# Larger load tiles for a row-projection and running-record kernel: 64 KB per partition in three slots instead of 48 KB in four

## The chip, the cores and the metric

The kernel runs on one core of one Trainium2 chip. The metric is device time in microseconds (us). The kernel before takes 631.44 us, the median of the six runs beside the changed kernel (631.24 to 631.77). All runs quoted here were of the state "fast". A packet is what one of the core's 16 DMA engines moves in one piece; here a partition's share of a tile is one packet (40 tiles of 128 partitions are the 5120 packets below). Where a number comes from the trace's DMA packet records and not from a printed view, I say so.

## The reference

```python
B, S, D = 8, 2048, 4096
def reference(x, w):                       # x [8, 2048, 4096], w [4096, 1], float32
    proj = (x @ w).squeeze(-1)             # [8, 2048]
    cm = np.maximum.accumulate(proj, axis=1)
    is_record = (proj >= cm).astype(np.float32)
    return np.cumsum(is_record, axis=1).astype(np.float32)
```

Every one of the 268 MB of `x` is used once, in a dot product of 4096 elements.

## The kernel before

The 2048 positions are cut into five groups of 384 (R = 3 rows for each of 128 partitions) and a tail of 128. For a group, eight tiles are loaded, one for each batch row. A tile is 128 partitions x 48 KB, and a partition's three rows lie side by side in memory. Four slots hold tiles. VectorE does the dot over columns 0 to 2816; GpSimd multiplies the other 1280 columns and ACT (ScalarE) sums them. TensorE turns the sums into one row per batch row, in PSUM, and VectorE scans that row.

```python
R = 3; NS = 4; NG = (S - P) // (R * P)
xbuf = [xall[:, i * R * D : (i + 1) * R * D] for i in range(NS)]
for k in range(NK):                                   # NK = NG * B tiles
    g, t = divmod(k, B)
    i = SY.dma_start(out=xbuf[k % NS], in_=x[B - 1 - t, g * N : (g + 1) * N, :]
            .rearrange("(p r) d -> p (r d)", r=R)).then_inc(xs[k % NS], 16)
    if k >= NS:
        i._wait_ge(fr[k % NS], 2 * (k // NS))         # VectorE and ACT are done with the slot
    # ... cut: weights, output of the group before
with V.Fori(0, NG):                                   # GpSimd and ACT have such loops too
    group_scans()
    V.sem_inc(psr, -3)
    V.sem_inc(od, -16)
    for t in range(B):
        b, s = B - 1 - t, t % NS
        V.wait_ge(xs[s], 16).then_inc(go, 1)
        V.sem_inc(xs[s], -16)
        for j in range(R):
            i = dot(xbuf[s][:, j * D : j * D + VC], w_v[:, :VC],
                    sum_v[:, j * B + b : j * B + b + 1])
        i.then_inc(fr[s], 1)
# ... cut: matmuls of each group; the tail: six whole rows, then nine ever smaller pieces
```

Of the kernel before, what the change touches and what calls it, by code (L numbers as in the profile page):

```python
# [13 lines left out]
ALU = mybir.AluOpType  # L14
ACTF = mybir.ActivationFunctionType
NEG = -3.0e38
LOW = -3.2e38
# [3 lines left out]
def kernel(  # L21
# [16 lines left out]
    P = 128  # L38
    B, S, D = x.shape
    WC = 512  # L40
    NW = D // WC
    R = 3
    NS = 4
    NG = (S - P) // (R * P)
    N = R * P
    S0 = NG * N
    assert S0 + P == S and B % NS == 0
    VC = 2816
    PC = D - VC
    CV = 3584  # L50
# [20 lines left out]
    def sb(shape, name, **kw):  # L71
        return pool.tile(shape, FP32, name=name, **kw)
# [5 lines left out]
    xbuf = [xall[:, i * R * D : (i + 1) * R * D] for i in range(NS)]  # L78
    w_sb = sb([P, PC], "w_sb")
    cm = sb([B, N], "cm")  # L80
    rec = sb([B, N], "rec")
    cnt = sb([B, N], "cnt")
    cm_l, rec_l, cnt_l = (sb([B, P], n) for n in ("cm_l", "rec_l", "cnt_l"))
    w_v = wpool.tile([P, CV], FP32, name="w_v")
    ps = wpool.tile([P, WC], FP32, name="ps")
    w_row = w2[:NW, :]
# [8 lines left out]
    sum_v, sum_p = cut(R * B), cut(R * B)  # L95
# [3 lines left out]
    acc_v, acc_p = accs[:, : len(PIECES)], accs[:, len(PIECES) :]  # L99
    fin = cut(1)  # L100
    neg = cut(1)[:B]
    zero = ps[:B, WC - 1 :]

    ns = iter(range(1000))

    def sem(name):
        return tc.alloc_semaphore(f"{name}_{next(ns)}")

    rows = [b for b in reversed(range(B)) if b > 1]
    xs = [sem("xs") for _ in range(NS)]  # L110
    fr = [sem("fr") for _ in range(NS)]
    xt = [sem("xt") for _ in rows]
    xq = [sem("xq") for _ in PIECES]
    ws, idn, bw, wc, cs, od, oe, psr, pd, pl, go, sd, pa, con = (
# [5 lines left out]
    def dot(xsl, wsl, dst):  # L120
        return V.tensor_tensor_reduce(  # L121
            out=xsl, in0=xsl, in1=wsl, scale=1.0, scalar=0.0,
            op0=ALU.mult, op1=ALU.add, accum_out=dst,
        )
# [7 lines left out]
        assert W2 <= c0 and c1 <= W2 + WC  # L132
        return w2[:, c0 - W2 : c1 - W2]

    def scans(cm_, rec_, cnt_, n, cm0, cnt0, base=1):
        V.tensor_tensor_scan(  # L136
            out=cm_, data0=ps[:B, :n], data1=neg.to_broadcast([B, n]), initial=cm0,
            op0=ALU.max, op1=ALU.max,
        )._wait_ge(psr, base).then_inc(psr, 1)
        V.tensor_tensor(  # L140
            out=rec_, in0=ps[:B, :n], in1=cm_, op=ALU.is_ge
        )._wait_ge(psr, base + 1).then_inc(psr, 1)
        V.tensor_tensor_scan(  # L143
            out=cnt_, data0=rec_, data1=zero.to_broadcast([B, n]), initial=cnt0,
            op0=ALU.add, op1=ALU.add,
        )._wait_ge(psr, base + 2).then_inc(cs, 1)

    NK = NG * B
    with tc.tile_critical(no_gpsimd_drain=True):  # L149

        for k in range(NK):
            g, t = divmod(k, B)
            i = SY.dma_start(
                out=xbuf[k % NS],
                in_=x[B - 1 - t, g * N : (g + 1) * N, :].rearrange(
                    "(p r) d -> p (r d)", r=R
                ),
            ).then_inc(xs[k % NS], 16)
            if k >= NS:
                i._wait_ge(fr[k % NS], 2 * (k // NS))  # L160
            if k == 0:
                A.dma_start(
                    out=w_row, in_=w.rearrange("(k c) one -> k (c one)", k=NW)
                ).then_inc(ws, 16)
            if t == NS and g:
                SY.dma_start(
                    out=out[:, (g - 1) * N : g * N], in_=cnt
                )._wait_ge(cs, g + 1).then_inc(od, 16)

        def slot(m):  # L170
            return m // R, xbuf[m // R][:, (m % R) * D : (m % R + 1) * D]

        freed = set()

        def row_load(m, c0, c1, b, done):
            s, xb = slot(m)
            i = SY.dma_start(
                out=xb[:, c0:c1], in_=x[b, S0:, c0:c1]
            ).then_inc(done, 16)
            if s not in freed:  # L180
                freed.add(s)
                i._wait_ge(fr[s], 2 * (NK // NS))

        for m, b in enumerate(rows):
            row_load(m, 0, D, b, xt[m])
        for i, (b, c0, c1, _, _) in enumerate(PIECES):
            row_load(B - 1 - b, c0, c1, b, xq[i])
            if i == 3:
                SY.dma_start(
                    out=out[:, (NG - 1) * N : S0], in_=cnt  # L190
                )._wait_ge(cs, NG + 1).then_inc(oe, 16)


# [10 lines left out]
        for n, k in enumerate(order):  # L204
            c = k * WC
# [16 lines left out]
        V.memset(cnt[:, N - 1 :], 0.0)  # L222
        V.wait_ge(con, 3)
        V.wait_ge(wc, 3)
        V.memset(ps[:B, :N], LOW)  # L225
        V.memset(zero, 0.0).then_inc(psr, 1)

        def group_scans():
            V.wait_ge(od, 16)
            scans(cm, rec, cnt, N, cm[:, N - 1 :], cnt[:, N - 1 :])  # L230

        with V.Fori(0, NG):
            group_scans()
            V.sem_inc(psr, -3)
            V.sem_inc(od, -16)
            for t in range(B):
                b, s = B - 1 - t, t % NS
                V.wait_ge(xs[s], 16).then_inc(go, 1)
                V.sem_inc(xs[s], -16)  # L239
                for j in range(R):  # L240
                    i = dot(
                        xbuf[s][:, j * D : j * D + VC], w_v[:, :VC],
                        sum_v[:, j * B + b : j * B + b + 1],
                    )
                i.then_inc(fr[s], 1)

        G.wait_ge(wc, 3)
        with G.Fori(0, NG):
            for t in range(B):
                s = t % NS  # L250
                for j in range(R):
                    xl = xbuf[s][:, j * D + VC : (j + 1) * D]
                    i = G.tensor_mul(out=xl, in0=xl, in1=w_sb).then_inc(pl, 1)  # L253
                    if j == 0:
                        i._wait_ge(go, 1)
                G.sem_inc(go, -1)  # L256

        with A.Fori(0, NG):
            for t in range(B):
                b, s = B - 1 - t, t % NS  # L260
                for j in range(R):
                    i = add_up(
                        xbuf[s][:, j * D + VC : (j + 1) * D],
                        sum_p[:, j * B + b : j * B + b + 1],
                    )._wait_ge(pl, j + 1)
                i.then_inc(fr[s], 1)
                A.sem_inc(pl, -R)
            A.wait_ge(pd, 1)
            A.sem_inc(pd, -1)

        for g in range(NG):
            for j in range(R):
                for k, l in enumerate((sum_p, sum_v)):
                    i = T.matmul(  # L274
                        out=ps[:B, j:N:R], lhsT=l[:, j * B : (j + 1) * B],
                        rhs=identity, start=k == 0, stop=k == 1,
                    )
                    if j == k == 0:
                        i._wait_ge(fr[NS - 1], 2 * (g + 1) * B // NS)
                    if j == R - 1:  # L280
                        i.then_inc((pd, psr)[k], 1)


# [3 lines left out]
        def piece(xb, v, p, dst_v, dst_p, landed):  # L287
            nonlocal nv, npool, na
            dot(xb[:, v[0] : v[1]], w_v[:, v[0] : v[1]], dst_v)._wait_ge(
                landed, 16  # L290
            ).then_inc(sd, 1)
            nv += 1
            if p:
                xl = xb[:, p[0] : p[1]]
                G.tensor_mul(out=xl, in0=xl, in1=w_pool(*p))._wait_ge(  # L295
                    landed, 16
                ).then_inc(pl, 1)
                npool += 1
                add_up(xl, dst_p)._wait_ge(pl, npool).then_inc(pa, 1)
                na += 1  # L300

        for m, b in enumerate(rows):
            piece(
                slot(m)[1], (0, VC), (VC, D), st_v[:, b : b + 1], st_p[:, b : b + 1],
                xt[m],
            )
            if m == 0:
                group_scans()
        for i, (b, c0, c1, v, p) in enumerate(PIECES):
            if b == 1:  # L310
                dst_v, dst_p = (b1x if p is None else st_v)[:, 1:2], st_p[:, 1:2]
            else:
                dst_v, dst_p = acc_v[:, i : i + 1], acc_p[:, i : i + 1]
            if i == len(PIECES) - 1:
                V.wait_ge(pa, na)
            piece(slot(B - 1 - b)[1], v, p, dst_v, dst_p, xq[i])
            if i == 1:
                parts += [(B, st_v, (sd, nv)), (B, b1x, None), (B, st_p, (pa, na))]
        V.tensor_reduce(
# [1 line left out]
        )._wait_ge(sd, nv).then_inc(sd, 1)  # L321
        nv += 1
        parts.append((1, fin, (sd, nv)))

        for k, (m, l, wait) in enumerate(parts):
            i = T.matmul(  # L326
                out=ps[:m, :P], lhsT=l[:, :m], rhs=identity,
# [2 lines left out]
            if wait:  # L330
                i._wait_ge(*wait)
        i.then_inc(psr, 1)
        scans(cm_l, rec_l, cnt_l, P, cm[:, N - 1 :], cnt[:, N - 1 :], 4)
        SY.dma_start(out=out[:, S0:], in_=cnt_l)._wait_ge(cs, NG + 2).then_inc(oe, 16)
        G.wait_ge(oe, 16 * 2)

# [29 lines left out]
```

## Time and profile before

| | before |
|---|---|
| time, median of 6 | 631.44 us |
| DMA share of 16 engines, x queue | 98.8% |
| VectorE, GpSimd busy | 65%, 59% |
| x packets of 48 KB: count, median duration | 5120, 1815 ns |
| first x byte moves, last x byte lands | 2.0, 623.2 us |

These lines of the page of the kernel before are the busy digits of the 40 slices, the rate, and the DMA queues (packets, MB, share of 16 engines' time).

```profile
DVE  0756666677655557766666675556667766655887
POOL 0555666666555555666666555556666666555865
DMA  9999999999999999999999999999999999999995
...
DMA packets 8034, 268.54 MB, mean 427 GB/s; under 512 B 936, under 2 KB 1496, under 8 KB 2016
...
q1 hardware_dynamic: 8016, 268.50, 98.8%
...
q14 instruction: 2, 0.02, 0.0%
```

The DMA row is full until the last slice while VectorE and GpSimd are not: the loads bound the kernel.

Next come stretches of the same kernel: window, length, busy time (and count) of each engine, TensorE clock, DMA share, GB/s. Then what the load queue waited for.

```profile
31.50:600.00 568.50, 13.64 (x60) 7.32 (x60) 370.88 (x252) 162.07 (x238) 343.31 (x120) 1.00 1.00 434
600.00:623.20 23.20, 1.61 (x6) 0.47 (x6) 21.11 (x23) 8.25 (x16) 16.09 (x7) 1.00 0.97 407
623.20:629.30 6.10, 0.59 (x2) 0.09 (x2) 2.38 (x10) 0.17 (x2) 0.00 (x0) 1.00 0.00 1
```

```profile
SPq L153 <- ACT xall L127: 519.5, 36, 27.6
SPq L177 <- ACT xall L127: 40.6, 3, 14.2
```

From 31 to 600 us the DMA share is 1.00 at 434 GB/s; after the last x byte 6.1 us remain. The queue's own waits for ACT (line, us in total, times, longest) look large, but with a DMA share of 1.00 they are harmless: loads are issued a few tiles ahead, and the next one simply waits for a slot.

### The profile page before, as it was taken

What the parts mean: (1) busy time and instruction counts of PE and PEld (TensorE: products, weight loads), DVE (VectorE), ACT (ScalarE), POOL (GpSimd) and SP (SyncE); (2) the same over time, 40 slices, a digit from 0 to 9 for tenths busy, and PEclk for the clock granted to TensorE, in tenths of its full rate; (3) what the DMA queues carried; (4) which work ended last, traced back from release to release, by engine and by line L of the source; (5) the groups of instructions that cost most, each with busy time, mean ns of one, the idle gap of its engine ahead of it and who ended that gap; (6) DMA issues with size and microseconds to landing.
All of it is one profiled execution on the core that took longest, in us unless ns stands there. A gap on an engine that the chain in (4) does not pass through costs nothing.

```text
span 629.3 us, 1209 instructions
## 1 busy us (share of the span) xinstructions
PE 29.8 (5%) x84; PEld 13.0 (2%) x84; DVE 406.4 (65%) x296; ACT 177.7 (28%) x262; POOL 369.1 (59%) x137
## 2 busy tenths in 40 slices
PE   8000000010000001000000010000001000000101
PEld 3000000000000000000000000000000000000000
DVE  0756666677655557766666675556667766655887
ACT  1322223233332222223232322222233232322332
POOL 0555666666555555666666555556666666555865
DMA  9999999999999999999999999999999999999995
GB/s 382 419 447 441 412 450 438 413 450 434 419 447 435 419 447 437 422 441 437 423 441 437 425 437 441 422 438 441 428 431 444 434 422 447 435 419 447 410 428 232
DMA packets 8034, 268.54 MB, mean 427 GB/s; under 512 B 936, under 2 KB 1496, under 8 KB 2016
## 3 DMA queue, kind: packets, MB, share of 16 engines
q1 hardware_dynamic: 8016, 268.50, 98.8%
q10 hardware_dynamic: 16, 0.02, 0.0%
q14 instruction: 2, 0.02, 0.0%
HBM read 268.45 MB, written 0.07 MB: 427 GB/s over the span
## 4 chain that ended last, share of the span: by engine, by line
POOL 53%; issue 39%; DMA 4%; PE 3%; DVE 1%; POOLq 0%; ACT 0%; SPq 0%; ACTq 0%
POOL xall L253 53%; DMA xall<-in_x_dram 3%; PE w_v L207 2%; PE ps L274 0%; DVE xall L121 0%; PE ps L207 0%; DMA w<-in_w_dram 0%; DVE cm L136 0%; DVE cnt L143 0%; POOLq L256 0%; PE ps L326 0%; ACT w L217 0%; DVE rec L140 0%; DVE cm_l L136 0%; DVE cnt_l L143 0%
## 5 line engine op out<-in xcount | busy, mean ns | idle before, releaser
L121 DVE CUSTOM_DVE_ANT_0 xall<-xall,w_v 128x2816 f32<-128x2816 f32 (+3 forms) x135 | 389.3, 2930 | 185.5 <-DVEq L239 183.4
L253 POOL TENSOR_TENSOR xall<-xall,w_sb 128x1280 f32<-128x1280 f32 x120 | 345.1, 2905 | 245.9 <-POOLq L256 245.9
L127 ACT ACTIVATE xall<-xall 128x1280 f32<-128x1280 f32 x129 | 162.6, 1261 | 430.6 <-POOL xall L253 412.7
L274 PE MATMUL ps<-identity,small 128*8 128x128 f32 x60 | 13.6, 417 | 566.7 <-ACT xall L127 566.7
L295 POOL TENSOR_TENSOR xall<-xall,w_sb 128x1280 f32<-128x1280 f32 (+1 forms) x8 | 22.1, 2763 | 6.7 <-DMA xall<-in_x_dram 6.7
L127 ACT ACTIVATION_READ_ACCUMULATOR xall<-xall 128x1 f32 x129 | 24.0, 186 | 0.0
L274 PEld LDWEIGHTS ps<-identity,small 128*8 128x8 f32 x60 | 7.3, 128 | 574.1 <-ACT xall L127 570.2
L136 DVE TENSOR_TENSOR_SCAN cm<-ps,cm,small 8x384 f32<-8x384 f32 x6 | 6.0, 1004 | 15.0 <-PE ps L274 14.9
L207 PE MATMUL w_v<-w,identity 8*128 8x512 f32 x14 | 12.2, 1056 | 0.0
L225 DVE MEMSET ps<- 8x384 f32 x1 | 0.4, 378 | 17.3 <-ACT w L217 17.3
L121 DVE DVE_READ_ACCUMULATOR2_ANT small<- 128x1 f32 x135 | 10.9, 81 | 0.0
L143 DVE TENSOR_TENSOR_SCAN cnt<-rec,cnt,ps 8x384 f32<-8x384 f32 x6 | 6.0, 1001 | 0.2
L207 PEld LDWEIGHTS w_v<-w,identity 8*128 8x128 f32 x14 | 4.7, 333 | 7.3 <-issue 7.3
L214 ACT COPY w_sb<-w_v 128x768 f32<-128x768 f32 x1 | 0.8, 800 | 11.4 <-PE w_v L207 11.4
L326 PE MATMUL ps<-identity,small 128*8 128x128 f32 (+1 forms) x8 | 2.2, 404 | 25.7 <-DVE small L121 22.9
L140 DVE TENSOR_TENSOR rec<-ps,cm 8x384 f32<-8x384 f32 x6 | 3.3, 546 | 0.2
L207 PE MATMUL ps<-w,identity 8*128 8x512 f32 x2 | 2.1, 1136 | 2.8 <-DMA w<-in_w_dram 2.8
L213 ACT ACT_TABLE_LOAD x1 | 1.3, 1283 | 1.6 <-SPq L149 1.6
L213 ACT COPY w_sb<-ps 128x512 f32<-128x512 f32 x1 | 0.6, 587 | 2.1 <-PE ps L207 2.1
L326 PEld LDWEIGHTS ps<-identity,small 128*8 128x8 f32 (+1 forms) x8 | 0.6, 99 | 27.3 <-DVE small L121 23.4
L295 POOL TENSOR_TENSOR xall<-xall,w 128x320 f32<-128x320 f32 x1 | 0.9, 867 | 0.1
L136 DVE TENSOR_TENSOR_SCAN cm_l<-ps,cm,small 8x128 f32<-8x128 f32 x1 | 0.5, 470 | 0.7 <-PE ps L326 0.7
(16 smaller groups left out, 3.6 us busy)
## 6 DMA issues: line engine op xcount, KB each, us to landing
xall<-in_x_dram SPq DMA_DIRECT2D x40, 6144.0 KB, 47.8
xall<-in_x_dram SPq DMA_DIRECT2D x6, 2048.0 KB, 42.8
xall<-in_x_dram SPq DMA_DIRECT2D x1, 1344.0 KB, 36.7
xall<-in_x_dram SPq DMA_DIRECT2D x2, 384.0 KB, 30.6
xall<-in_x_dram SPq DMA_DIRECT2D x1, 704.0 KB, 38.0
xall<-in_x_dram SPq DMA_DIRECT2D x1, 640.0 KB, 39.1
xall<-in_x_dram SPq DMA_DIRECT2D x1, 224.0 KB, 21.9
xall<-in_x_dram SPq DMA_DIRECT2D x1, 192.0 KB, 21.9
```

The source lines that it names most:

```text
L121: return V.tensor_tensor_reduce(out=xsl, in0=xsl, in1=wsl, scale=1.0, scalar=0.0, op0=ALU.mult, op1=ALU.add, accum_out=dst,)
L127: return A.activation(out=xsl, in_=xsl, func=ACTF.Copy, accum_out=dst)
L136: V.tensor_tensor_scan(out=cm_, data0=ps[:B, :n], data1=neg.to_broadcast([B, n]), initial=cm0, op0=ALU.max, op1=ALU.max,)._wait_ge(psr, ba ...
L140: V.tensor_tensor(out=rec_, in0=ps[:B, :n], in1=cm_, op=ALU.is_ge)._wait_ge(psr, base + 1).then_inc(psr, 1)
L143: V.tensor_tensor_scan(out=cnt_, data0=rec_, data1=zero.to_broadcast([B, n]), initial=cnt0, op0=ALU.add, op1=ALU.add,)._wait_ge(psr, base ...
L207: i = T.matmul(out=dst, lhsT=identity[:NW, k : k + 1].to_broadcast([NW, P]), rhs=w_row, start=True, stop=True,).then_inc(bw, 1)
L213: A.copy(out=w_sb[:, CV - VC :], in_=ps)._wait_ge(bw, 1).then_inc(wc, 1)
L214: A.copy(out=w_sb[:, : CV - VC], in_=w_v[:, VC:CV])._wait_ge(bw, NW).then_inc(wc, 1)
L253: i = G.tensor_mul(out=xl, in0=xl, in1=w_sb).then_inc(pl, 1)
L274: i = T.matmul(out=ps[:B, j:N:R], lhsT=l[:, j * B : (j + 1) * B], rhs=identity, start=k == 0, stop=k == 1,)
L295: G.tensor_mul(out=xl, in0=xl, in1=w_pool(*p))._wait_ge(landed, 16).then_inc(pl, 1)
L326: i = T.matmul(out=ps[:m, :P], lhsT=l[:, :m], rhs=identity, start=k == 0, stop=k == len(parts) - 1,)
```

## The change

The intent is fewer, larger packets. 1536 positions come in three groups of 512, with 64 KB per partition and tile, in three slots; the last 384 positions come in tiles of the old size that begin at the third slot. That leaves 16 KB free at the top of every slot, and three tail rows go there. The three engine loops cannot hold the odd last group as it is, so it is written out as straight code behind each loop. Two small edits ride along: the record flags overwrite the scores in PSUM, and the last sum's wait moves behind the last dot. Semaphores now go by tile of a group and not by slot. The title of the change also names "one final matmul"; the code has four closing matmuls before and after.

```diff
-    R = 3
-    NS = 4
-    NG = (S - P) // (R * P)
+    RS = (4, 4, 4, 3)
+    R = RS[0]
+    NS = 3
+    NG = len(RS)
+    NL = NG - 1
...
+    def at(g, t):
+        return xbuf[(t if g < NL else t + NS - 1) % NS]
+    def user_before(g, t):
+        if t >= NS:
+            return t - NS, g + 1
+        if g == NL:
+            return B - NS + t, g
+        return max(u for u in range(B) if u % NS == t), g
...
+                    out=at(g, t)[:, : r * D],
+                    in_=x[B - 1 - t, STARTS[g] : STARTS[g] + r * P, :].rearrange(
+                        "(p r) d -> p (r d)", r=r
...
-        with V.Fori(0, NG):
-            group_scans()
+        def next_group():
+            group_scans()
             V.sem_inc(psr, -3)
             V.sem_inc(od, -16)
+        with V.Fori(0, NL):
+            next_group()
+            group_dots(R)
+        next_group()
+        group_dots(RS[-1], NL)
... (the same for GpSimd and ACT)
         def slot(m):
-            return m // R, xbuf[m // R][:, (m % R) * D : (m % R + 1) * D]
+            if m < NS:
+                return None, xbuf[m][:, RS[-1] * D :]
+            u = B - NS if m < 2 * NS else B - NS + 1
+            return u, at(NL, u)[:, (m % NS) * D : (m % NS + 1) * D]
...
+            piece(slot(B - 1 - b)[1], v, p, dst_v, dst_p, xq[i])
             if i == len(PIECES) - 1:
                 V.wait_ge(pa, na)
-            piece(slot(B - 1 - b)[1], v, p, dst_v, dst_p, xq[i])
```

## The prediction

> **What bounds it now.** The loads of x. In the 40 slices the DMA engines are 90% busy or more in all but the last; queue 1 takes 98.8% of 16 engines' span. Between 31.5 and 600 us (busy time by stretch) the DMA share is 1.00 at 434 GB/s, while VectorE works 371 and GpSimd 343 of 568 us. The Trainium skill ("DMA: Bandwidth & Descriptors", section "Where 436 GB/s comes from") puts the ceiling at 435.2 GB/s; this trace agrees. In the DMA packet records the 5120 packets of 48 KB last 1815 ns (median), the 768 of 16 KB 611 ns; 384-row tiles end 14.506 us apart. The first byte of x moves at 2.0 us, the last at 623.2; then come 6.1 us of last dot, matmul, three small scans and store. The chain of waits names GpSimd and "issue", but those are waits for landed tiles.
>
> **What the change does.**
> 1. Packets. 1536 positions come in 24 tiles of 128 x 64 KB instead of 32 of 128 x 48 KB; the other 512 load in the same shapes. From 611 and 1815 ns a packet costs about 9 ns plus 1204 ns per 32 KB; so 64 KB should take about 2417 ns, and a tile 19.33 us. Each engine handles 64 packets fewer: 0.6 us. By tile-to-tile times (14.506 us for eight 48 KB, 4.862 for eight 16 KB) the saving is 0.3 us. I take 0.4.
> 2. Slots: four of 48 KB become three of 64 KB. A tile is freed four dots (4 x 3.01 us) and the last ACT sum after landing, some 13.5 us; the two tiles behind it hold 38.7 us of transfer: slack about 25 us (before: 43.5 - 10.5 = 33). The DMA does not run dry. At a group's end matmuls (8 x 0.42 us) and scans (2.55 us scaled to 512 columns: 3.4) delay the next dots by about 8 us, inside the slack.
> 3. Work per row is the same: 135 dots, 120 GpSimd products, 129 sums. One scan set fewer and no zero memset; the record flags go in place into PSUM. All is hidden under the loads except the last scans (0.47, 0.28, 0.47 us), where PSUM may change 0.1 us.
> 4. Tail: three of the six whole rows use the free upper 16 KB of the slots and are issued one to two tiles earlier. The queue is full there anyway (the SP queue is held up to 8.6 us issuing pieces), so nothing lands earlier. The moved wait for the sums costs nothing. The diff leaves four closing matmuls, so the title's "one final matmul" removes nothing.
>
> **On the critical path:** only item 1, -0.3 to -0.6 us, and ±0.2 us of the tail. Predicted 631.0 us, 0.1% less; range 629.8 to 632.6. Chances: faster by over 2% 0.01, within 2% 0.95, slower by over 2% 0.04.
>
> **What would show it.** 3072 packets of 65536 bytes at about 2417 ns; tiles 19.33 us apart; DMA share 1.00 from 31 to 600 us; last x byte at about 622.8 us; 6.1 us from there to the end; the SP queue's main wait still ACT freeing a slot.
>
> **What would make it wrong.** (a) A 64 KB run might be cut into two packets: 3072 more at 9 ns over 16 engines, 1.7 us. (b) Rows of neighbouring partitions then lie 64 KB apart, a power of two. The skill's same page (section "Latency and other measured facts", HBM row pitch) reports losses at pitches of 512 KiB and above; the tail's 16 KB pitch shows none here (611 ns flat). If 64 KB did, packets would exceed 2417 ns: the slow 4%. (c) Slots come free late and gaps appear between tiles; the DMA share would fall below 1.00.

## The result, and the profile after

| | before | after |
|---|---|---|
| time, median of 6 (range) | 631.44 us (631.24 to 631.77) | 631.46 us (631.31 to 632.14) |
| x packets of the large tiles | 5120 of 48 KB, 1815 ns | 3072 of 64 KB, 2418 ns; 1024 of 48 KB, 1815 ns |
| time from tile to tile (median) | 14.500 us | 19.319 us (64 KB) |
| last x byte lands | 623.20 us | 623.83 us |
| from there to the end of the span | 6.07 us | 5.71 us |
| span of the profiled run | 629.27 us | 629.55 us |
| span, mean (9 and 5 runs of one chip, with e11) | 629.44 us | 629.76 us |
| time less span, mean of the same | 2.08 us | 1.79 us |

The ratio after over before is 1.0002, with a 95% interval of 0.9989 to 1.0015. A ratio is the mean time of one kernel's fast runs over that of the other's of the same rounds, so it is not quite the ratio of the medians quoted. The prediction of 631.0 us with a range of 629.8 to 632.6 holds, but the 0.4 us that it forecast did not appear. The last two rows show that "no change" is a sum: on that chip the span of the program grew by 0.32 us, and what the time counts outside the span shrank by 0.29. One longer run of the five (632.11 us) carries much of the 0.32; on the chip of e1 the same two figures are 0.10 and 0.22.

The same parts of the changed kernel's page (the clock row is printed because it was below 1):

```profile
DVE  0755676456785557755579655677557966555887
POOL 0555676456765557755567655577555966555855
PEclk9999999999975555555555555555555555555555
DMA  9999999999999999999999999999999999999995
...
DMA packets 6868, 268.55 MB, mean 427 GB/s; under 512 B 800, under 2 KB 1328, under 8 KB 1872
...
q1 hardware_dynamic: 6848, 268.50, 98.8%
q14 instruction: 4, 0.03, 0.0%
```

The same stretches, and the queue's waits:

```profile
31.50:600.00 568.50, 13.43 (x60) 7.53 (x60) 370.59 (x251) 163.58 (x240) 343.21 (x121) 0.63 1.00 434
600.00:623.80 23.80, 1.62 (x6) 0.48 (x6) 20.98 (x23) 8.11 (x13) 15.89 (x7) 0.50 0.94 394
623.80:629.50 5.70, 0.58 (x2) 0.09 (x2) 2.37 (x10) 0.21 (x2) 0.00 (x0) 0.50 0.00 1
```

```profile
SPq L163 <- ACT xall L128: 537.3, 27, 39.0
SPq L191 <- ACT xall L128: 26.0, 2, 13.2
```

The packets fell from 8016 to 6848, the rate stayed at 434 GB/s and the DMA share at 1.00. The stretch after 600 us is where something is off: it is 0.6 us longer, and its DMA share is 0.94 instead of 0.97. The drop is that of the added 0.6 us alone, in which few engines still work: cut at 623.2 us, the changed kernel shows 0.97 too.

```profile
600.00:623.20 23.20, 1.62 (x6) 0.48 (x6) 20.38 (x21) 7.52 (x11) 15.68 (x7) 0.50 0.97 404
```

So a mean over 16 engines does not tell whether one of them is late. And the instruction packets are four instead of two. The granted TensorE clock (PEclk) dropped to about half early in this run. TensorE is far from the bound, and the straight-code run below took 631.33 us at a clock of 1.0 and 631.34 at 0.609, so the clock explains nothing.

**What the packet records say.** In the changed kernel four packets of 8 KB of the instruction queue lie among the loads, at 104.4, 116.6, 492.3 and 602.6 us; the kernel before has two, at 95.3 and 119.0 us. Each takes 309 ns or so on one of the 16 DMA engines, and the x packet behind it is stretched (takes longer than its like) too: the one after the packet at 602.6 us takes 1141 ns instead of 611. Together that holds one DMA engine up by 0.84, 0.55, 0.53 and 0.84 us. Nothing evens this out: each engine has its own share of every tile queued (8 of the 128 partitions), so an engine that is late stays late, and the pieces of the tail wait for the latest engine. The last dot that waited for a load is this one, before and after:

```profile
620.86 0.95 DVE L121 CUSTOM_DVE_ANT_0 xall<-xall,w_v 128x768 f32<-128x768 f32 x1 [0.27 <-DMA xall<-in_x_dram]
621.53 0.95 DVE L122 CUSTOM_DVE_ANT_0 xall<-xall,w_v 128x768 f32<-128x768 f32 x1 [0.22 <-DMA xall<-in_x_dram]
```

From there VectorE works without a wait until the last dot. It starts 0.67 us later in the changed kernel, and the last x byte lands 0.63 us later, so the last x byte serves as a mark for the end of the loads. To measure lateness I take when each of the 16 engines ends the sixth whole tail row, and subtract the median engine from the latest.

| | median engine | latest | latest minus median | last x byte |
|---|---|---|---|---|
| before | 612.33 us | 613.10 | 0.77 | 623.20 |
| after | 612.17 us | 613.74 | 1.57 | 623.83 |

So the median engine did gain 0.16 us in these two profiles, and the latest engine lost 0.64. (In the profiles of the changed kernel in e1 and e11 the median engine ended at 612.5 and 611.9 us, so a gain of this size varies from run to run.) The moment of the loss can be seen: in the changed kernel the latest engine is 0.72 us behind the median at the end of the third whole row (598.3 us) and 1.56 at the end of the fourth (604.0 us). The packet at 602.6 us fell on the engine that was the latest already. In e1, e6, e8 and e11 the lag also grows by 0.84 us in this row, and in e9, which has no packet there, it does not grow.

**Theory.** The larger packets save what the tile spacing says, about 0.3 us for each DMA engine. Straight code behind the loops brings a second fetch of VectorE's code, which falls on the DMA engine that carried its first fetch, late in the loads. It puts that engine 0.84 us further back, and this eats the saving, so that the span does not shrink. **Rivals.** The late engine was chance; packet size does not matter because the total rate is at its limit; the 64 KB distance between partitions' rows costs; or three slots leave too little ahead.

### The profile page after: what moved, and what is told of

It reads as the page before. It is cut to its first block, busy times and chain, and to the rows that moved or that the text cites. A ratio compares the mean times of both kernels' runs of the same rounds, so it can differ in the third digit from the quotient of the medians.

```text
span 629.5 us, 1144 instructions
## 1 busy us (share of the span) xinstructions
PE 29.7 (5%) x84; PEld 13.2 (2%) x84; DVE 406.2 (65%) x292; ACT 177.8 (28%) x262; POOL 368.8 (59%) x137
## 3 DMA queue, kind: packets, MB, share of 16 engines
q1 hardware_dynamic: 6848, 268.50, 98.8%
## 4 chain that ended last, share of the span: by engine, by line
POOL 52%; issue 37%; DMA 7%; PE 2%; DVE 1%; SPq 0%; POOLq 0%; ACT 0%; ACTq 0%
POOL xall L273 52%; DMA xall<-in_x_dram 6%; PE w_v L221 2%; DVE xall L122 0%; PE ps L221 0%; SPq L191 0%; DMA w<-in_w_dram 0%; POOLq L276 0%; ACT w L231 0%; PE ps L354 0%; DVE cm_l L138 0%; DVE cnt_l L144 0%; DVE ps L141 0%; ACT xall L128 0%; DVE small L348 0%
## 5 line engine op out<-in xcount | busy, mean ns | idle before, releaser
L138 DVE TENSOR_TENSOR_SCAN cm<-ps,cm,small 8x512 f32<-8x512 f32 (+1 forms) x5 | 6.1, 1217 | 13.5 <-PE ps L303 13.4
L144 DVE TENSOR_TENSOR_SCAN cnt<-ps,cnt,small 8x512 f32<-8x512 f32 (+1 forms) x5 | 6.1, 1217 | 0.2
L141 DVE TENSOR_TENSOR ps<-ps,cm 8x512 f32<-8x512 f32 (+1 forms) x5 | 3.3, 660 | 0.2
```

What stands on the lines that cost most here:

```text
L138: V.tensor_tensor_scan(out=cm_, data0=ps[:B, :n], data1=low, initial=cm0, op0=ALU.max, op1=ALU.max,)._wait_ge(psr, base).then_inc(psr, 1)
L141: V.tensor_tensor(out=ps[:B, :n], in0=ps[:B, :n], in1=cm_, op=ALU.is_ge)._wait_ge(psr, base + 1).then_inc(psr, 1)
L144: V.tensor_tensor_scan(out=cnt_, data0=ps[:B, :n], data1=low, initial=cnt0, op0=ALU.add, op1=ALU.max,)._wait_ge(psr, base + 2).then_inc(cs, 1)
```

## The experiments

Eleven runs, all correct, were timed in five rounds each, on three chips. The median of before was 631.52 us in the first four, 631.42 in the next four and 631.55 in the last three.

### e1_again: the changed kernel unaltered

> The changed kernel again, unaltered, for a second profile and a tighter interval. Theory (packets saved, given back by instruction fetches): tiles of 64 KB again 19.32 us apart; four 8 KB instruction packets, two of them in the peeled code (near 492 and 602 us); each stretches one x packet by 0.2 to 0.5 us and takes 0.31 us itself, on one of the 16 DMA engines; if the same engine is last again, the last x byte comes at about 623.8 us, else at 622.8 to 623.0. Time 631.2 to 631.8. Rival (chance alone): the late engine of the first profile was an accident of that run, and the 16 engines now end within 0.4 us of one another, as before.

Measured: 631.43 us, ratio to before 0.9997 (0.9983 to 1.001). Instruction packets at 106.8, 116.3, 492.7 and 602.9 us; last x byte at 624.20 us; latest minus median 1.59 us. The late engine is no accident of one run. (That the engines ended "within 0.4 us of one another" before is a slip in that text: the latest was 0.77 behind the median.)

### e2_peeled: the kernel before, last group as straight code

```diff
-        with V.Fori(0, NG):
-            group_scans()
+        def v_group():
+            group_scans()
...
+        with V.Fori(0, NG - 1):
+            v_group()
+        v_group()
... (the same for GpSimd and ACT)
```

> The kernel before, 48 KB tiles in four slots, with only its last group taken out of the three loops and written out as straight code, as the change does. Fetch theory: one or two more 8 KB instruction packets after 480 us, each delaying one DMA engine by 0.5 to 0.8 us; time 631.4 to 632.2, that is 0 to 0.8 us over the kernel before. Rival: straight code costs nothing and the saving of the change is lost elsewhere; no more instruction packets, time within 0.1 us of before.

Measured: 631.33 us, ratio 0.9997 (0.9983 to 1.001). One more instruction packet came during the loads (516.5 us) and held one engine up 0.53 us, and the next one came only at 628.2 us, after the loads. Last x byte 623.46 us, 0.27 later than before in one profile of each. The time is not higher: straight code need not cost anything; by the theory it depends on where the fetches fall. By the letter of the theory's expectation (0 to 0.8 us more) this is a miss within the noise; the run does not decide. It did show a second effect: from the last x byte to the end took 5.68 us, as in the changed kernel, and not 6.07. In the records, the kernel before has 0.39 us between GpSimd's last but one drain and the clearing of the semaphores, and these two have 0.03. In other ways it is like the kernel before: its time is 2.10 us over its span. I take both ends for further effects of where code lies (before and this run have an instruction packet at 631.0 to 631.1 us, after their spans; the changed kernel's traces have none), but tested no cause.

### e3_pad: the kernel before with 1280 idle instructions on TensorE

```diff
+        for _ in range(2560):          # two such waits share an instruction
+            T.wait_ge(idn, 1)
         for g in range(NG):
```

> The kernel before with 1280 more instructions on TensorE's sequencer (waits that are already met), placed where TensorE waits for the first group anyway. 80 KB of code is ten fetches of 8 KB. If the fetches of one engine's code all go over one DMA engine, x packets on it are held up 10 x 0.53 to 10 x 0.84 us: time up by 5 to 8 us. If they are spread over the 16 DMA engines: up by 0.5 to 0.8 us. If fetches cost x nothing: within 0.2 us of before, with ten more packets to be seen.

Measured: 632.70 us, ratio 1.0017 (1.0004 to 1.0031), 1.2 us more. The page of this run:

```profile
q1 hardware_dynamic: 8016, 268.50, 98.6%
q8 instruction: 5, 0.08, 0.0%
```

TensorE's code came in five packets of 16 KB, in another queue, not ten of 8 KB. Each held an x packet's engine up 1.43 us (0.9 us for itself, 0.5 us of stretch). Neither of my two sums came out (5 to 8, or 0.5 to 0.8 us). All five on one engine would be 7.1 us; spread evenly, 0.45. The last x byte came 1.43 us later than in the profile of before. What follows is only that code fetches do cost time when the DMA engines are the bound, and that these five did not all fall on the latest engine.

### e4_rows and e5_blocks: the same bytes in 16 KB packets

e4: one transfer for each row of a partition; neighbouring partitions read 64 KB apart.

```diff
-                i = SY.dma_start(
-                    out=at(g, t)[:, : r * D],
-                    in_=x[B - 1 - t, STARTS[g] : STARTS[g] + r * P, :].rearrange(
-                        "(p r) d -> p (r d)", r=r
-                    ),
-                ).then_inc(xs[t], 16)
+                for j in range(r):
+                    i = SY.dma_start(
+                        out=at(g, t)[:, j * D : (j + 1) * D],
+                        in_=x[B - 1 - t, STARTS[g] + j : STARTS[g] + r * P : r, :]
+                    ).then_inc(xs[t], 16)
```

> The changed kernel, each tile loaded by one transfer per row of a partition (16 KB packets, still 64 KB apart for neighbouring partitions) instead of one transfer with 64 KB packets. 32 tiles: 640 more packets for each DMA engine (24 x 8 x 3 + 8 x 8 x 2 = 704, less none). Packet theory: each costs 5.3 ns (from the tile-to-tile times 4 x 4.862 - 19.319 us, over 24 packets) to 9 ns (from packet durations): time up by 3.7 to 6.3 us on the changed kernel. Rival: packet size makes no difference to the total[...]; within 0.5 us.

(The count in that text is muddled; 24 x 8 x 3 + 8 x 8 x 2 = 704 more packets for each engine is right.) Measured: 635.09 us, 3.6 us more than the changed kernel, ratio to before 1.0055 (1.0041 to 1.0069). 3.6 us over 704 packets is 5.1 ns for a packet. It is a little low, since e4's packets had none of the slow stretches of 64 KB packets that step 1 below tells of. Packet size does count, and the tile spacing (5.3 ns) had the right figure. The durations in the records (9 ns) overstate it, because successive packets of an engine overlap by some 4 ns there. 64 fewer packets are worth 64 x 5.1 ns = 0.33 us.

e5: the same, but row j of partition p is position 128 j + p, so neighbouring partitions read 16 KB apart.

```diff
-                        in_=x[B - 1 - t, STARTS[g] + j : STARTS[g] + r * P : r, :]
+                        in_=x[B - 1 - t, STARTS[g] + j * P : STARTS[g] + (j + 1) * P, :]
...
-                        out=ps[:B, j : r * P : r], lhsT=l[:, j * B : (j + 1) * B],
+                        out=ps[:B, j * P : (j + 1) * P], lhsT=l[:, j * B : (j + 1) * B],
```

> As the run with one transfer per row (16 KB packets), but a tile's row j of partition p is now position j x 128 + p, so that neighbouring partitions read rows 16 KB apart instead of 64 KB; the matmul writes its columns side by side to match. If the 64 KB distance cost anything, this is faster than its sister (635.09 us) by over 0.5 us. If distance does not matter: within 0.3 us of it, packets of 611 ns throughout in both.

Measured: 635.45 us, ratio to its own before 1.0065 (1.0052 to 1.0079), on another chip than e4. It is slightly slower than e4, not faster, by 0.36 us where I had allowed 0.3 (each against its own before, by 0.46: 4.03 against 3.57); packets last 611 ns (median) in both. The 64 KB distance costs nothing in packets of 16 KB; for packets of 64 KB it was not tested.

### e6_twoback: the third slot never used ahead

```diff
+                if g < NL and (g or t > 1):
+                    SY.wait_ge(fr[(t - 2) % B], 2 * (g + (t > 1)))
                 i = SY.dma_start(
```

> The changed kernel, each 512-row load also waiting until the tile two before it is used up, so that the third slot is never used ahead. At a group's boundary the changed kernel does this already (the first tile of the next group takes the slot of the tile two before it), with 5.8 us of transfer left in the queue. If 5.8 us is enough, tiles stay 19.32 us apart and the time is within 0.3 us of the changed kernel's. If the three-deep queue is needed, a gap of 1 us or more opens at each of 21 tiles: 20 us or more slower.

Measured: 631.35 us, ratio 1.0001 (0.9987 to 1.0014); tiles 19.319 us apart (median). One tile behind the one in use is enough while tiles are 64 KB, so the smaller number of slots cost nothing in the changed kernel, which leaves no less than this.

### e7_looped: last group kept in the loops

```diff
     def at(g, t):
-        return xbuf[(t if g < NL else t + NS - 1) % NS]
+        return xbuf[t % NS]
...
-        with V.Fori(0, NL):
-            next_group()
-            group_dots(R)
-        next_group()
-        group_dots(RS[-1], NL)
+        with V.Fori(0, NG):
+            next_group()
+            group_dots(R)
... (the same for GpSimd and ACT; the tail rows go to slots 2 and 0)
```

> The changed kernel with the last group kept in the loops: its tiles are 384 rows but the engines work through four rows of each (the fourth is old data, its sums are not used), slots in the order of the other groups, tail rows in the slots that come free. VectorE's code is 144 instructions instead of 215, so its second 8 KB fetch, near 602 us, should go, and ACT's near 492 us too. Fetch theory: the DMA engine that is 1.6 us behind the middle of the 16 is then 0.84 us behind; last x byte at 622.9 to 623.2 instead of 623.8 and 624.2; time 630.5 to 631.0, 0.5 to 0.9 us under the changed kernel's. Rival (the late engine is late for another reason): last x byte and time as in the changed kernel, within 0.2 us.

Measured: 632.95 us, ratio 1.0027 (1.0014 to 1.0041): slower, not faster. VectorE's second fetch was indeed gone (instruction packets at 106.8, 116.4 and 589.7 us). But two new costs came. The second tile of the last group ended 16.13 us after the first instead of 14.50. And the work on old rows put VectorE behind: its last dot began 0.96 us after the last x byte, not 0.61. The run tests two things at once, which was poor design; e9 and e10 part them.

### e8_vpad: one more fetch of VectorE's code

```diff
         V.memset(ps[:B, :N], LOW).then_inc(psr, 1)
+        for _ in range(256):           # 128 instructions
+            V.wait_ge(con, 3)
```

> The changed kernel with 128 more instructions (met waits) on VectorE ahead of its loop, which shift its code by one fetch of 8 KB. Fetch theory: one more VectorE fetch, on the same DMA engine as the others of VectorE; that engine ends 0.84 us later than in the changed kernel: last x byte 624.6 to 625.1, time 632.0 to 632.5. Rival: a further fetch falls on another engine or costs nothing, and the time stays within 0.2 us of the changed kernel's.

Measured: 632.18 us (631.95 to 632.38), 0.75 us over the changed kernel's 631.43 (e1, on another chip; e8 is 0.76 over its own before, e1 0.09 under), ratio to before 1.0012 (0.9998 to 1.0025). Instruction packets at 27.0, 105.4, 116.5, 492.4 and 603.5 us; last x byte 624.80; latest minus median 2.44 us. As expected.

### e9_lean: 16 instructions fewer in VectorE's straight code

```diff
+                if g < NL:
                     V.wait_ge(xs[t], 16).then_inc(go, 1)
                     V.sem_inc(xs[t], -16)
                 for j in range(r):
                     i = dot(...)
+                    if g == NL and j == 0:
+                        i._wait_ge(xs[t], 16)
... (GpSimd: in the last group its first product waits on xs[t], not on go, and the count-down of go is left out)
```

> The changed kernel with 16 instructions fewer in VectorE's straight code: in the last group the first dot and the first product of a tile wait for the load themselves, instead of a wait and a count-down on VectorE and a go signal to GpSimd. From the runs so far VectorE's code is fetched again some 128 instructions after the first fetch; with 16 fewer that point should slip from tail row 2 or 3 (602.6 us) to the last pieces, after or at the end of the x loads. Fetch theory: no instruction packet between 495 and 622 us, the latest DMA engine 0.84 us behind the middle one instead of 1.6; last x byte 622.8 to 623.3; time 630.5 to 631.0, 0.5 to 0.9 us under the changed kernel on the same chip. Rival: last x byte and time as in the changed kernel, within 0.2 us.

Measured: 630.67 us (630.59 to 630.91), ratio to before 0.9986 (0.9973 to 1.0). The changed kernel on the same chip took 631.48 us (631.33 to 632.11), before 631.55 (631.26 to 631.72); the ranges do not meet. The mean span is 628.94 us, against 629.76 of the changed kernel and 629.44 of before. There is no instruction packet between 472.8 us and 628.2 us. Latest minus median is 0.74 us, and the last x byte comes at 623.38 us (expected 622.8 to 623.3). The late fetch is worth 0.81 us, and this version was faster than both kernels, by 0.13% and 0.14% (the interval of the ratio to before just reaches 1). Of its 0.88 us over before (medians), some 0.29 lie outside the span and 0.3 after the last x byte (5.74 us instead of 6.07 in the profiles), so the larger packets by themselves are worth at most the few tenths that are left. The profile shows not even these: its last x byte lands 0.18 us after that of before. It is of the slowest of the five runs, and slow 64 KB packets cost more in it than in any other profile (0.69 us, step 1 below).

### e10_slot0: last group beginning at the first slot

```diff
     def at(g, t):
-        return xbuf[(t if g < NL else t + NS - 1) % NS]
+        return xbuf[t % NS]
     def user_before(g, t):
         if t >= NS:
             return t - NS, g + 1
-        if g == NL:
-            return B - NS + t, g
```

> The changed kernel with the last group's tiles beginning at the first slot, as the other groups' do, not at the third. Its second tile then waits until the tile just before the group is used up, 13.5 us after landing, with only one 384-row tile (14.5 us) in the queue. Slot theory: a gap of about 1.6 us in the loads at the second tile of the last group, as in the looped run, and a time of 632.8 to 633.2 us, 1.4 to 1.7 us over the changed kernel. Rival (the gap of the looped run came of its extra work on old rows): tiles 14.5 us apart, time within 0.3 us of the changed kernel.

Measured: 632.43 us (632.17 to 632.61), 0.95 us over the changed kernel, ratio to before 1.0015 (1.0001 to 1.0028). The stretches around that tile, of this run:

```profile
470.00:480.00 10.00, 0.00 (x0) 0.00 (x0) 10.00 (x7) 4.54 (x7) 9.52 (x4) 1.00 1.07 462
480.00:484.00 4.00, 3.03 (x15) 1.97 (x16) 0.29 (x2) 0.92 (x2) 0.00 (x0) 1.00 0.69 221
484.00:490.00 6.00, 0.55 (x3) 0.06 (x1) 5.34 (x4) 0.13 (x1) 3.07 (x2) 0.84 1.00 434
```

And of the changed kernel:

```profile
470.00:480.00 10.00, 0.00 (x0) 0.00 (x0) 10.00 (x7) 4.49 (x7) 9.57 (x4) 0.50 1.07 462
480.00:484.00 4.00, 2.98 (x15) 1.92 (x16) 0.35 (x2) 0.96 (x2) 0.00 (x0) 0.50 0.97 418
```

The DMA share falls to 0.69 for 4 us, and the tile comes 16.10 us after the one before: the gap is real and is that of the looped run (there too 221 GB/s in this stretch). The load was issued at 480.94 us, 1.1 us before the tile ahead of it ended at 482.07, and that is too late to keep the engines fed. In the changed kernel both boundaries between 64 KB groups have 5.8 to 6.0 us instead (152.53 us against 158.36, 307.03 against 313.00), and no gap. "Begin at the third slot" is what keeps the loads going. The cost was less than the 1.4 to 1.7 us I wrote, because in the gap the late engine catches up: latest minus median is 0.75 us at the end, one fetch, not two.

### e11_again: the changed kernel on the chip of the last two

> The changed kernel once more, on the same chip as these two, for a comparison in the same rounds and a third profile: 631.2 to 631.7 us, last x byte 623.8 to 624.2, VectorE's second instruction packet near 602.6 us, and 1.5 to 1.6 us from the middle DMA engine to the latest.

Measured: 631.48 us, ratio 1.0 (0.9987 to 1.0014). Last x byte 623.96 us, VectorE's second packet at 602.7 us, latest minus median 1.93 us, somewhat more than I wrote.

## Why the prediction was right or wrong, point by point

**The bound: right.** DMA share 1.00 and 434 GB/s in both. The Trainium skill ("DMA: Bandwidth & Descriptors", section "Where 436 GB/s comes from") gives 435.2 GB/s for the 16 ports into the on-chip memory; both traces agree. The same section says that for transfers between HBM and that memory the HBM side, about 358 GB/s, binds; the 434 GB/s of these loads from HBM do not agree with that.

**Step 1, packets: right in mechanism, half of the size reasoning wrong.** There are 3072 packets of 64 KB at 2418 ns (predicted 2417), not cut in two, and tiles are 19.319 us apart (predicted 19.33). The saving is the smaller of my two sums, 0.33 us (e4), not 0.6. Not foreseen: in every profile of kernels with 64 KB packets some of them run slow for a stretch, mostly 30 to 130 ns over 2418, at changing times between 34 and 305 us. Averaged over the 16 engines this cost 0.40 us in the changed kernel, 0.56 and 0.13 in its repeats, 0.39 in e6, 0.69 in e9, and about 0.05 or less in the three profiles of kernels with 48 KB packets alone. It takes back the packets' gain in most runs. In e4 and e5, with 16 KB packets at 64 and 16 KB distance, it cost 0.00 us, so the distance alone does not bring it. Whether it is the size, or the distance at this size, no run tells: this stays open.

**Step 2, slots: conclusion right, number wrong.** I wrote that the two tiles behind leave "slack about 25 us". That holds inside a group. At a boundary the slot order restarts, the first tile of a group takes the slot of the tile two before it, and 5.8 us are left. e6 shows that this suffices, e10 that 1.1 us does not.

**Step 3, engine work: right.** VectorE 406.4 us before and 406.2 after; the last scans in PSUM took 0.47, 0.29 and 0.47 us.

**Step 4, the tail: incomplete, and this is the step that failed.** The prediction put "only item 1, -0.3 to -0.6 us, and ±0.2 us of the tail" on the critical path and expected the last x byte at 622.8 us; it came at 623.83. I counted the straight code as nothing. The count of VectorE fetches on the latest engine explains the runs:

| run | VectorE fetches during the loads | latest minus median | last x byte | time |
|---|---|---|---|---|
| before | 1 | 0.77 us | 623.20 us | 631.44 us |
| e9_lean | 1 | 0.74 | 623.38 | 630.67 |
| after; e1; e6; e11 | 2 | 1.57; 1.59; 1.74; 1.93 | 623.83; 624.20; 623.98; 623.96 | 631.46; 631.43; 631.35; 631.48 |
| e8_vpad | 3 | 2.44 | 624.80 | 632.18 |

Each fetch adds 0.84 us by the records, and the lag and, within the changed kernel and its variants, the time follow; before has one fetch too, but its longer end. (e7 and e10 are left out for their gap in the loads.) That a fetch belongs to VectorE and that they share a DMA engine is inferred, from where each engine stands in its code, from these sums, and from the stretch of the x packet behind: it is 0.53 to 0.54 us for the packets at 104.4 and 602.6 us and for the one that e8 adds at 27.0 us, and 0.22 to 0.24 us for those at 116.6 and 492.3 us. That 16 or 128 instructions of VectorE's move the time by -0.8 or +0.75 us is shown. So the step that failed is the bound of ±0.2 us on the tail: a code fetch late in the loads, on the engine that was latest already, cost 0.84 us there. The Trainium skill describes the road ("DMA: Bandwidth & Descriptors", section "Queues, rings and completion order"): a runtime-internal row of queues for refill and others sits on the same 16 engines, which take packets from the rows in turn. The records agree, with an 8 KB packet of 309 ns on queue 14 between two x packets; TensorE's code in e3, however, came by queue 8.

**The end: not foreseen.** The prediction expected 6.1 us after the last x byte; it took 5.71. So in the two profiles the balance is -0.16 us for the median engine, +0.80 for the late engine and -0.36 at the end: +0.28 us of span (629.27 to 629.55). Outside the span 0.29 us fell away, and the medians differ by 0.02. I had no term for either end. That the two shrank is measured; why is not. That the total still came within 0.5 us of my 631.0 is in part luck: the late fetch and the slow stretches took away more than the packets saved, and two shorter ends that I had not thought of gave it back.

**The risks named.** A 64 KB run was not cut. The distance of 64 KB costs nothing in e4 against e5. The skill's same page (section "Latency and other measured facts", HBM row pitch) reports losses from 512 KiB on; no run here reaches that. Gaps between tiles did not appear in the changed kernel.

## What to carry to other kernels

When all DMA engines are full, anything else that they carry can add to the time, code fetches too (0.8 us here, and nothing in e2): after writing a loop out as straight code, count the instruction packets in the profile and see where in the loads they fall, for a few instructions fewer may move one out of the way. The time is set by the latest of the 16 engines, so look at the spread between them and not only at their mean share. When slots rotate and loops restart the rotation, work out the slack at the boundary, not inside.

## What the Trainium skill lacked or had wrong

- "Runtime: NRT & Kernel Launch", section "Instruction fetch mechanics", says that code is refilled in blocks of 16 KiB and that the cost is mostly hidden. Here TensorE's code came in 16 KB packets (e3), but the fetches of VectorE's and the other loops' code came in packets of 8 KB. And in a kernel bound by the loads they are not hidden when they fall on the latest engine: a fetch held one DMA engine up by 0.53 to 0.84 us (8 KB) or 1.43 us (16 KB), and e9 against e11 is 0.81 us of time. In e2 one more fetch during the loads (0.53 us, at 516.5 us) left the time as it was.
- No page says that a code fetch makes one DMA engine late, and that the delay stays until the queue runs dry: the lag was 0.74, 1.6 to 1.9 and 2.4 us with one, two and three fetches.
- "DMA: Bandwidth & Descriptors" has no time for what a large packet costs beside its bytes (its section "Why small descriptors are slow (HBM only)" gives a fixed overhead of about 3 cycles for each packet). Here it was 5.1 ns for each from 64 KB down to 16 KB (704 packets, 3.6 us). It has none either for the stretches in which 64 KB packets run mostly 30 to 130 ns slow.
- The same page does not say how late a load may be issued behind another: 1.1 us of transfer left in the queue gave a gap of 1.6 us, 5.8 us gave none.
